# One layer in FP32: the first norm and its first twenty products as one region in a written order, the set-up placed later, and the values of both attention branches projected together

## The chip, the cores and the metric

The kernel runs on one core of one Trainium2 chip. The metric is the device time of one execution in microseconds (us); the median of several executions is given. Engines are called as in the profile: PE (TensorE, matmul; PEld are its weight loads, which overlap the matmuls), DVE (VectorE), ACT (ScalarE), POOL (GpSimd) and SP (SyncE, which issues most DMAs).

## The reference

The layer takes x (1024 tokens by 1024 columns, FP32) and computes

```
x = x + 1/2 * SwiGLU_1(RMSNorm(x))            # d_ff 2816
u = RMSNorm(x);  proj = u @ w_mix_in          # q,k,v of branch A, q,k,v of branch B, gate logits
A = chunked band attention (8 heads of 64)    # B = differential attention (4 heads, v of 128)
x = x + W_o( sigmoid(g_A) * (A W_A) + sigmoid(g_B) * (B W_B) )
x = x + 1/2 * SwiGLU_2(RMSNorm(x))
out = RMSNorm(x)
```

with `rms_norm(x, g) = x * rsqrt(mean(x*x) + eps) * g` and `swiglu(x) = (silu(x @ w_gate) * (x @ w_up)) @ w_out`. The values of the branches, `v_a` and `v_b`, are 512 columns of the projection each.

## The kernel before

Each large matrix product is done in a Strassen-like form: both operands are cut into 2 x 2 blocks and seven products (`PRODUCTS`, numbered m = 0 to 6) replace eight. The token side needs seven operands (`U_OPS`: A11, A12, S1 to S4, A22; S1 = A21 + A22, S2 = S1 - A11, S3 = A11 - A21, S4 = A12 - S2), the weight side four blocks and the differences T1, T2, T3, N4. Each FP32 operand is split (`split`, L97 and L102) into a rounded high part, cast by ACT, and a low part, subtracted by DVE; each block product is then three matmuls (`mm3`, L128 to L130: high by high, high by low, low by high).

A `Pair` takes two 128-column strips of an input projection (for the first SwiGLU one strip of the gate half and one of the up half). One product of a pair is four blocks of 128 rows, so 12 matmuls of 512 token columns. Its accumulators are chains in PSUM: chain "q" runs through m = 0, 3, 5, 6, "r" through 1 and 4, "s" is m = 2. `Combine` copies and adds what leaves the chains and hands the four result blocks to a sink. `ffn_in` has 22 pairs. The first five (`HEADS`) are begun with m = 0 and m = 2 alone (`head`), since these need only A11 and A12, the upper half of the tokens; the remaining products follow in `rest`, pair by pair. The sink applies silu to gate blocks (L401), multiplies (L409), and stores hidden blocks and their sums to DRAM; of a begun pair's gate block one is parked in DRAM (`begun`, `gb`).

The first norm, at the start, is in the code below: for each of eight row tiles of 128 tokens the row is loaded, ACT squares it with a running sum (`take`, L174), DVE adds eps (L180), POOL takes the power -1/2 (L139), DVE scales by root and gain (L181), PE transposes (L208), ACT and DVE split (`norm0`, `norm1a` to `norm1c`).

`setup` is a generator that `ffn_in` steps at pairs 5, 8, 11 and 14: lambda's four vectors and their dots (L651, L654), `subln_g`, the gate bias (transposed), then the tables of the two relative biases (POOL, L644) written to DRAM, which the attention stage reads. Its loads are issued on POOL's queue. `tc.issue_after(...)` around a step queues only its instructions of ACT's own queue behind the given silu.

`project_v` is called twice from `mixer_in`, once per branch, with one pair between. Each call cuts the 512 value columns into two of 256; the tokens are the stationary operand, the weights move, 256 columns at a time.

The order of the instructions on each engine is made by the framework's scheduler from data dependences, priorities and its own time estimate; nothing before the change is ordered by hand at the start. A region under `tc.manual_schedule(engines=...)` keeps, on each engine named, the order in which the code issues them; where other instructions fall among them is still the scheduler's. Buffers are rings by tag: ten raw tiles (`raw`), ten weight units (`w`, two for each split block), ten `f` temporaries, three `t`; PSUM has six `mm` banks and two `tr`.

Of the kernel before, what the change touches and what calls it, by code (L numbers as in the profile page):

```python
# [9 lines left out]
F32 = mybir.dt.float32  # L10
F32R = mybir.dt.float32r
AF = mybir.ActivationFunctionType
ALU = mybir.AluOpType
# [3 lines left out]
P = 128  # L17
# [28 lines left out]
WA = 640  # L46
EA = 768
WB = 1024
HEADS = 5
SKEW = 32  # L50
EB = 1152
# [3 lines left out]
def hybrid_layer_kernel(ctx, tc, x, ffn1_norm, ffn1_w_in, ffn1_w_out, mix_norm, w_mix_in,  # L55
# [306 lines left out]
            pass  # L362


    def ffn_in(w_in, u, ps, extra=None):
# [24 lines left out]

        begun = drams(HEADS, [P, HALF], "gb")
        keeps = []

        def make_sink(j):
            keep = {}
            keeps.append(keep)

            def sink(th, blk, ap):
                if blk == 0:
                    dst = temp([P, HALF], "gate") if th else ap  # L400
                    silu.append(nc.scalar.activation(out=dst, in_=ap, func=AF.Silu))  # L401
                    ap = dst
                if j < HEADS and (th, blk) == (0, 0):
                    nc.sync.dma_start(out=begun[j], in_=ap)
                    return
                keep[th, blk] = ap
                if (th, 0) in keep and (th, 1) in keep:
                    hid[j, th] = h = keep[th, 1]
                    nc.vector.tensor_tensor(out=h, in0=h, in1=keep[th, 0], op=ALU.mult)  # L409
                    hidden(j, th)  # L410
            return sink

        pairs = [Pair(w_in, j * P, FF + j * P, u, ps, make_sink(j)) for j in range(NF)]
        for p in pairs[:HEADS]:
            p.head()
            yield
        for j, p in enumerate(pairs):
            if j < HEADS:
                keeps[j][0, 0] = load(begun[j], temp([P, HALF], "gb"))
            if extra and j in (5, 8, 11, 14):  # L420
                with tc.issue_after(silu[-1].ins):
                    next(extra, None)
            p.rest()
# [214 lines left out]
    def setup(ps):  # L638

        def stage(shape, name):  # L640
            return sb.tile(shape, F32, tag="gain", bufs=1, name=name)
# [2 lines left out]
            nc.gpsimd.tensor_scalar(out=dst, in0=src, scalar1=-1.0, scalar2=None, op0=ALU.mult)  # L644


        for q, k in ((lambda_q1, lambda_k1), (lambda_q2, lambda_k2)):
            qk = []
            for v in (q, k):
                vt = small.tile([P, B_DIM], F32, tag="lv", bufs=2, name="lv")  # L650
                nc.gpsimd.dma_start(out=vt, in_=v[0].partition_broadcast(P))  # L651
                qk.append(vt)
            dot = small.tile([P, 1], F32, tag="dot", name="dot")
            nc.vector.tensor_tensor_reduce(out=qk[0], in0=qk[0], in1=qk[1], scale=1.0, scalar=0.0,  # L654
                                           op0=ALU.mult, op1=ALU.add, accum_out=dot)
            lams.append(dot)
        nc.gpsimd.dma_start(out=gsub, in_=subln_g[0].rearrange("(p o) -> p o", o=1))
        nc.gpsimd.tensor_scalar(out=gsub, in0=gsub, scalar1=1.0 - LAMBDA_INIT, scalar2=None, op0=ALU.mult)
        bg_rows = stage([16, P], "bg_rows")
        nc.gpsimd.dma_start(out=bg_rows, in_=b_gate[0].rearrange("(j p) -> j p", p=P))  # L660
# [14 lines left out]
        yield  # L675
        ea = stage([P, EA], "ea")
        n_clip = EA - (2 * REL_CLIP + 1)
        nc.gpsimd.dma_start(out=ea[:, n_clip:], in_=spread(rel_bias_a[0], A_HEADS, 2 * REL_CLIP + 1))
# [5 lines left out]
        nc.gpsimd.dma_start(out=tb, in_=spread(t5_bias, B_HEADS, 32))  # L684
# [9 lines left out]
    with tc.tile_pool(name="ps1", bufs=1, space=PSUM) as ps:  # L694

        u = new_u(U_OPS)
        ones = const.tile([1, P], F32, name="ones")
        nc.vector.memset(ones, 1.0)
        gain = sb.tile([P, D], F32, tag="gain", bufs=1, name="gain")
        for part in range(2):  # L700
            g_row = wtemp([1, HALF], "g_row")
            nc.scalar.dma_start(out=g_row, in_=ffn1_norm[0][part * HALF:(part + 1) * HALF].rearrange("(o d) -> o d", o=1))
            pg = ps.tile([P, HALF], F32, tag="mm", bufs=6, name="pg")
            nc.tensor.matmul(pg, ones, g_row, start=True, stop=True)
            nc.scalar.copy(out=halves(gain)[part], in_=pg)
        ffn1 = ffn_in(ffn1_w_in[0], u, ps, setup(ps))
        row0, row1 = [], []
        for t in range(4):
            row0.append(Row(load(rows(x)[t], raw_tile([P, D], "xt"))))
            row0[t].take()  # L710
            row0[t].scale(gain)
            norm0(t, row0[t], u, ps)
        next(ffn1, None)
        for t in range(4):
            row1.append(Row(load(rows(x)[4 + t], raw_tile([P, D], "xt"))))
            row1[t].take()
            row1[t].scale(gain)
            norm1a(t, row0[t], row1[t], u, ps)
        for _ in range(3):
            next(ffn1, None)  # L720
        for t in range(4):
            norm1b(t, row0[t], row1[t], u)
        next(ffn1, None)
        for t in range(4):
            norm1c(t, row1[t], u)
        run_all(ffn1)


        u2 = {}

        def project_v(br, c0):

            rw = [load(w_cols(w_mix, c0, HALF, 2 * r, 2), raw_tile([P, 2, HALF])) for r in range(4)]
            gets = [weight_ops({"B11": rw[q][:, :, :256], "B12": rw[q][:, :, 256:],
                                "B21": rw[2 + q][:, :, :256], "B22": rw[2 + q][:, :, 256:]},
                               [P, 2, 256]) for q in range(2)]

            def make_sink(a):
                def sink(th, blk, ap):
                    t0 = 4 * th + 2 * a  # L740
                    if (th, blk) == (1, 0):
                        o = temp([P, 2, 256], "vo")
                        nc.scalar.copy(out=o, in_=ap)
                        ap = o
                    nc.sync.dma_start(out=v_d[br][t0 * P:(t0 + 2) * P, blk * 256:(blk + 1) * 256].rearrange(
                        "(s p) c -> p s c", p=P), in_=ap)
                return sink
            ch = [Combine(ps, [P, 2, 256], make_sink(a)) for a in range(2)]
            for ms in ((0, 1), (2, 3), (4, 5), (6,)):
                ops = {}  # L750
                for a in range(2):
                    for m in ms:
                        an, bn, _ = PRODUCTS[m]
                        if a == 0:
                            ops[m] = [g(bn) for g in gets]
                        acc, first = ch[a].acc(m)
                        for s in range(2):
                            c = slice((2 * a + s) * P, (2 * a + s + 1) * P)
                            for k in range(4):

                                mm3(acc[:, s, :], [v[:, k, c] for v in u2[an]],
                                    [v[:, k % 2, :] for v in ops[m][k // 2]],
                                    first and s == 0 and k == 0, k == 3, not (first and s == 0))
                        ch[a].after(m, acc)

        def qk_sink(n):
            def sink(th, blk, ap):
# [18 lines left out]
        def mixer_in():  # L786
# [337 lines left out]
```

## Time and profile before

| what | value |
|---|---|
| time, median of 3 runs | 2111.92 us (2109.3 to 2114.98) |
| the profiled execution | 2110.54 us, its span 2108.7 us |
| mean granted TensorE clock | 0.994 |
| DMA | 324.61 MB, 153 GB/s of HBM over the span |

The span is the time between the first and the last instruction in the trace; the execution's own time lies a little above it. Rows of the trace name the line of the kernel, the engine and operation, and the tile written `<-` the tiles read.

### The profile page before, as it was taken

Reading aid. Unit: us, or ns where it says so; the run is one execution under the profiler, and the core shown is the slowest. Engines: PE = TensorE matmul, PEld = TensorE weight load, DVE = VectorE, ACT = ScalarE, POOL = GpSimd, SP = SyncE. Lnnn points to the kernel's source line nnn. Section 1 sums busy time; section 2 is a strip of 40 time slices with the busy share of each in tenths; the row PEclk is TensorE's granted clock in tenths of the full one; section 3 lists DMA queues with packets and bytes.
Section 4 is the critical chain, followed back from the end, with each engine's and each line's share of the span. In section 5 each row is a group of like instructions: output and inputs, shape, how many; then the busy total and the mean of one; then the engine's idle time right before and its main releaser. Section 6 shows DMA issues by size and latency. Waiting matters only on the chain.

```text
span 2108.7 us, 28259 instructions
## 1 busy us (share of the span) xinstructions
PE 2044.7 (97%) x9901; PEld 1699.8 (81%) x9901; DVE 1379.2 (65%) x2462; ACT 956.5 (45%) x1828; POOL 140.3 (7%) x202
## 2 busy tenths in 40 slices
PE   6899999999999999999999999999899999999998
PEld 4688888888888788899877888788688888888887
DVE  6765656658567855654656787568765656658566
ACT  6433333334446644433467666157433333334454
POOL 2300000000000000000036211000000000000000
PEclk9999999999999999999999999999999999999999
DMA  5743423366344744643495265734543323376335
GB/s 164 217 135 100 125 85 106 104 249 225 96 139 136 205 135 130 230 150 115 140 318 181 106 200 179 245 122 131 177 136 100 124 86 101 109 248 226 95 109 177
DMA packets 274580, 324.61 MB, mean 154 GB/s; under 512 B 15246, under 2 KB 170654, under 8 KB 274436
## 3 DMA queue, kind: packets, MB, share of 16 engines
q1 hardware_dynamic: 273248, 319.55, 46.4%
q0 software_dynamic: 1184, 3.24, 0.6%
q8 instruction: 78, 1.28, 0.2%
q14 instruction: 66, 0.54, 0.1%
q10 hardware_dynamic: 4, 0.00, 0.0%
HBM read 221.74 MB, written 100.99 MB: 153 GB/s over the span
## 4 chain that ended last, share of the span: by engine, by line
PE 88%; DVE 6%; issue 2%; ACT 2%; DMA 1%; POOL 0%; SPq 0%; POOLq 0%; DVEq 0%; ACTq 0%
PE prod L128 19%; PE prod L129 19%; PE prod L130 19%; PE po L129 7%; PE po L128 7%; PE po L130 7%; PE pt L859 2%; DVE wlo L102 1%; PE pv L943 1%; PE pb L128 1%; PE pb L129 1%; PE pb L130 1%; PE sc L843 1%; PE sc L844 1%; DVE B L113 1%
## 5 line engine op out<-in xcount | busy, mean ns | idle before, releaser
L129 PE MATMUL po<-wlo,whi 128*128 128x512 f32 x700 | 273.8, 391 | 1.8 <-DVE wlo L102 1.8
L130 PE MATMUL po<-whi,wlo 128*128 128x512 f32 x700 | 272.5, 390 | 0.0
L97 ACT CAST whi<-raw 128x512 fp32r<-128x512 f32 x200 | 124.1, 622 | 293.6 <-PE prod L129 223.7
L97 ACT CAST whi<-T 128x512 fp32r<-128x512 f32 x192 | 119.1, 622 | 260.5 <-PE prod L129 248.0
L113 DVE TENSOR_TENSOR c<-prod,c 128x512 f32<-128x512 f32 x190 | 130.9, 690 | 146.1 <-PE prod L130 132.6
L97 ACT CAST whi<-B 128x512 fp32r<-128x512 f32 x175 | 109.0, 623 | 243.4 <-PE po L129 236.3
L102 DVE TENSOR_TENSOR wlo<-T,whi 128x512 fp32r<-128x512 f32 x192 | 131.8, 688 | 115.8 <-ACT whi L97 104.3
L102 DVE TENSOR_TENSOR wlo<-B,whi 128x512 fp32r<-128x512 f32 x175 | 120.4, 688 | 128.4 <-ACT whi L97 128.4
L102 DVE TENSOR_TENSOR wlo<-raw,whi 128x512 fp32r<-128x512 f32 x200 | 137.4, 688 | 92.7 <-ACT whi L97 59.9
L128 PE MATMUL po<-whi 128*128 128x512 f32 x700 | 189.5, 390 | 0.0
L129 PEld LDWEIGHTS po<-wlo,whi 128*128 128x128 f32 x700 | 131.5, 188 | 30.9 <-DVE wlo L102 4.0
L130 PEld LDWEIGHTS po<-whi,wlo 128*128 128x128 f32 x700 | 131.5, 188 | 27.0
L128 PEld LDWEIGHTS po<-whi 128*128 128x128 f32 x700 | 131.1, 188 | 27.2 <-ACT whi L97 0.2
L139 POOL TENSOR_TENSOR r<-v,neg_half 128x1 f32<-128x1 f32 x32 | 26.4, 830 | 1363.7 <-DVE v L180 1291.6
L102 DVE TENSOR_TENSOR wlo<-N,whi 128x512 fp32r<-128x512 f32 x64 | 44.2, 690 | 108.4 <-PE prod L129 69.0
L102 DVE TENSOR_TENSOR wlo<-ha,whi 128x512 fp32r<-128x512 f32 (+1 forms) x157 | 105.7, 674 | 11.7 <-ACT whi L97 11.5
L287 ACT COPY c<-prod 128x512 f32<-128x512 f32 x186 | 102.1, 585 | 17.2 <-issue 10.5
L97 ACT CAST whi<-ha 128x512 fp32r<-128x512 f32 (+1 forms) x157 | 95.2, 608 | 25.5 <-PE po L129 13.0
L128 PE MATMUL prod<-A11h,whi 128*128 128x512 f32 x240 | 96.1, 401 | 7.9 <-DVE c L113 6.7
L853 ACT ACTIVATE pm<-pm,mn 128x640 f32<-128x640 f32 (+7 forms) x128 | 93.9, 735 | 20.3 <-DVE mn L851 17.6
L128 PE MATMUL prod<-A12h,whi 128*128 128x512 f32 x240 | 94.6, 394 | 3.4 <-DVE c L113 3.4
L851 DVE CUSTOM_DVE_ANT_0 pm<-sc,nb 128x640 f32<-128x640 f32 (+7 forms) x128 | 87.5, 701 | 14.9 <-PE sc L844 9.6
(245 smaller groups left out, 5108.0 us busy)
## 6 DMA issues: line engine op xcount, KB each, us to landing
raw<-in_ffn_w_in_dram SPq DMA_DIRECT2D x98, 512.0 KB, 4.2
raw<-in_w_mix_in_dram SPq DMA_DIRECT2D x47, 512.0 KB, 4.6
ha<-hS SPq DMA_DIRECT2D x88, 256.0 KB, 2.6
hA<-c SPq DMA_DIRECT2D x66, 256.0 KB, 4.2
ha<-hA SPq DMA_DIRECT2D x55, 256.0 KB, 2.7
B<-in_ffn_w_out_dram SPq DMA_DIRECT2D x12, 1024.0 KB, 12.1
hS<-hs SPq DMA_DIRECT2D x44, 256.0 KB, 2.4
hS<-c SPq DMA_DIRECT2D x44, 256.0 KB, 4.2
```

What stands on the lines that cost most here:

```text
L97: nc.scalar.copy(out=hi, in_=src)
L102: (nc.gpsimd if on_pool else nc.vector).tensor_tensor(out=lo, in0=src, in1=h, op=ALU.subtract)
L113: nc.vector.tensor_tensor(out=out_, in0=a, in1=b, op=op)
L128: nc.tensor.matmul(ps, a[0], b[0], start=first, stop=False, skip_group_check=shared)
L129: nc.tensor.matmul(ps, a[0], b[1], start=False, stop=False, skip_group_check=shared)
L130: nc.tensor.matmul(ps, a[1], b[0], start=False, stop=last, skip_group_check=shared)
L139: nc.gpsimd.tensor_tensor(out=r, in0=v, in1=neg_half, op=ALU.pow)
L287: nc.scalar.copy(out=self.held[name], in_=p)
L843: nc.tensor.matmul(sc[:, m, :wc], qs[:, h, c], ks[:, h, kc], start=True, stop=False)
L851: nc.vector.tensor_tensor_reduce(out=d3, in0=sc, in1=nb.rearrange("p (n w) -> p n w", n=n), scale=1.0, scalar=3e38, op0=ALU.add, op1=ALU.m ...
L853: nc.scalar.activation(out=dst, in_=dst, func=AF.Exp, bias=mn, scale=-1.0, accum_out=rs)
L859: nc.tensor.transpose(pt[:, b, :], p, ident)
```

## The change

In `ffn_in`, a function `begin` does the first norm, the two products of each of the five begun pairs and all other products of pairs 0 and 1, in the order of a written list of tokens; the loop skips a pair that has nothing left to do. Each token is one step: `sq:t` square, `rt:t` root, `sc:t[:n]` scale (of half n, for rows 0 to 3), `tr`/`tm:t:n` transpose half n into a `tr` or `mm` bank, `hi`/`lo` the split of A11 or A12, `kp` the copy of a turned half, `s1` to `s4` the sums, `hX`/`lX` the split of operand X, `wh`/`wl:n:m` the split of pair n's weight of product m, `t:n:m` its difference, `p:n:m` product m of pair n, `copy`, `add`, `out` what leaves the accumulators, `open:n` the loads of pair n's four blocks, `gate:n` the parked gate block. The sum with eps is now POOL's, the copies of the gain DVE's, and the gain's spread over 128 partitions uses two rows of the identity instead of a row of ones.

```diff
@@ constants
+BEGIN = """
+pg:0 pg:1 g:0 sq:0 rt:0 g:1 sq:1 rt:1 sc:0:0 sq:2 rt:2 sc:0:1 tr:0:0 sc:1:1 sq:3 rt:3 tr:0:1
+sc:1:0 hi:0:0 tm:1:1 sc:2:0 wh:0:0 lo:0:0 tm:1:0 hi:0:1 sc:3:1 kp:0:0 tm:2:0 lo:0:1 wh:1:0 sq:4
+rt:4 sc:2:1 tr:3:1 wl:0:0 tm:2:1 kp:2:0 sc:3:0 kp:1:0 wl:1:0 tm:3:0 hi:2:0 sc:4 kp:3:1 hi:1:0
+lo:2:0 hi:3:0 tm:4:1 hi:2:1 lo:1:0 tm:4:0 hi:3:1 lo:3:0 kp:4:1 lo:3:1 p:1:0 sq:6 rt:6 s1:0
+lo:2:1 wh:2:0 s3:0 wh:2:2 wl:2:0 hi:1:1 sc:6 sq:5 rt:5 p:0:0 wh:3:2 lo:1:1 kp:3:0 wl:2:2 wh:4:2
+wl:3:2 wh:4:0 tr:6:1 sc:5 p:3:2 wh:1:2 sq:7 rt:7 wl:4:0 s2:0 hS1:0 kp:2:1 lS1:0 tm:5:1 hS2:0
+wl:1:2 tm:5:0 kp:0:1 lS2:0 kp:5:1 tr:6:0 s3:1 wh:3:0 p:1:2 s3:2 hS3:0 hS3:1 sc:7 kp:6:1 kp:1:1
+s1:2 copy:1:0 tr:7:0 s1:1 hS1:2 p:2:0 add:1:2 hA22:2 s3:3 hS1:1 out:1:2 lS1:2 hS3:3 lS1:1 hA22:1
+lS3:3 p:2:2 copy:2:0 lA22:1 wh:0:2 wl:3:0 copy:0:0 wl:0:2 hA22:0 hS3:2 s2:2 p:3:0 lS3:0 hS2:2
+s4:2 lS2:2 hS4:2 add:2:2 s2:1 tr:7:1 out:2:2 p:0:2 wl:4:2 copy:3:0 s4:1 kp:7:1 open:0 hS2:1
+add:3:2 hS4:1 s1:3 out:3:2 lS2:1 p:4:2 hS1:3 s2:3 hA22:3 add:0:2 hS2:3 t:0:5 wh:0:4 out:0:2
+gate:0 t:0:1 p:4:0 lS2:3 t:0:3 wh:0:5 lS1:3 wh:0:3 wl:0:4 wh:0:1 wl:0:3 copy:4:0 wl:0:1 p:0:3
+add:4:2 wl:0:5 out:4:2 lA22:2 s4:0 p:0:1 lS4:1 copy:0:3 lS3:2 hS4:0 lS3:1 lA22:3 lS4:0 p:0:5
+copy:0:1 s4:3 open:1 gate:1 lA22:0 hS4:3 lS4:2 lS4:3 t:0:6 p:0:4 add:0:5 out:0:5 wh:0:6 t:1:1
+wh:1:4 wl:0:6 wh:1:1 t:1:3 p:0:6 wl:1:1 wh:1:3 wl:1:4 wl:1:3 t:1:5 t:1:6 p:1:3 wh:1:5 add:0:4
+out:0:6 wh:1:6 wl:1:5 out:0:4 wl:1:6 p:1:1 copy:1:3 p:1:5 copy:1:1 p:1:4 add:1:5 out:1:5 p:1:6
+add:1:4 out:1:4 out:1:6
+"""
@@ ffn_in
         pairs = [Pair(w_in, j * P, FF + j * P, u, ps, make_sink(j)) for j in range(NF)]
-        for p in pairs[:HEADS]:
+        if begin:
+            begin(pairs, keeps, begun)
+        for p in pairs[:0 if begin else HEADS]:
             p.head()
             yield
         for j, p in enumerate(pairs):
+            if not p.todo:
+                continue
@@ the start
+            def root(t):
+                v, r = (small.tile([P, 1], F32, tag=n, name=n) for n in "vr")
+                nc.gpsimd.tensor_scalar(out=v, in0=row[t].ssq[:, 0:1], scalar1=EPS, scalar2=None, op0=ALU.add)
+                nc.gpsimd.tensor_tensor(out=r, in0=v, in1=neg_half, op=ALU.pow)
+                row[t].r = r
...
+            def open_pair(n):
+                r1, r2 = (pairs[n].load(i) for i in range(2))
+                blocks[n] = {"B11": r1[:, :4], "B21": r1[:, 4:], "B12": r2[:, :4], "B22": r2[:, 4:]}
+                src[n, 4] = blocks[n]["B22"]
...
+            def weight_hi(n, m):
+                ops[n, m] = [unit([P, 4, P], v) for v in ("whi", "wlo")]
+                nc.scalar.copy(out=ops[n, m][0], in_=src[n, m])
...
+            def multiply(n, m):
+                acc[n, m], first = pairs[n].sums.acc(m)
+                for k in range(4):
+                    mm3(acc[n, m], [v[:, k, :] for v in ops[n, m]], [v[:, k, :] for v in u[PRODUCTS[m][0]]],
+                        first and k == 0, k == 3, not first)
+                pairs[n].todo.remove(m)
...
+            with tc.manual_schedule(engines={getattr(mybir.EngineType, e)
+                                             for e in ("Activation", "DVE", "PE", "Pool", "SP")}):
+                open_rows(0, 1, 2, 3)
+                half_load(0, 0)
+                half_load(1, 0)
+                open_rows(4, 5)
+                half_load(0, 2)
+                half_load(1, 2)
+                open_rows(6, 7)
+                half_load(2, 0)
+                half_load(2, 2)
+                for n in (3, 4):
+                    r = pairs[n].load(0)
+                    src[n, 0], src[n, 2] = r[:, :4], r[:, 4:]
+                for token in BEGIN.split():
+                    op, *args = token.split(":")
+                    do[op](*map(int, args))
```

In `setup` all loads move from POOL's queue to ACT's and so fall under `issue_after`; the first step now only loads, the dots, `gsub` and the gate bias come with the second.

```diff
+        rows_ = []
         for q, k in ((lambda_q1, lambda_k1), (lambda_q2, lambda_k2)):
             for v in (q, k):
-                vt = small.tile([P, B_DIM], F32, tag="lv", bufs=2, name="lv")
-                nc.gpsimd.dma_start(out=vt, in_=v[0].partition_broadcast(P))
+                vt = small.tile([P, B_DIM], F32, tag="lv", bufs=4, name="lv")
+                nc.scalar.dma_start(out=vt, in_=v[0].partition_broadcast(P))
+                rows_.append(vt)
+        nc.scalar.dma_start(out=gsub, in_=subln_g[0].rearrange("(p o) -> p o", o=1))
...
+        nc.scalar.dma_start(out=bg_rows, in_=b_gate[0].rearrange("(j p) -> j p", p=P))
+        yield
```

The values of both branches are one 2 x 2 block form with the branches as the two column blocks, called once; each matmul moves 512 columns. One product needs the split weights of four row blocks, eight units.

```diff
+            rw = {(r, c): load(w_cols(w_mix, (VA, VB)[c], HALF, 2 * r, 2), raw_tile([P, 2, HALF]))
+                  for r, c in ((0, 0), (1, 0), (2, 0), (3, 0), (0, 1), (1, 1), (2, 1), (3, 1))}
...
+            for m in (0, 2, 1, 4, 3, 5, 6):
+                an, _, chain = PRODUCTS[m]
+                w = [split_units(weight(m, k)) for k in range(4)]
+                for t in range(4):
+                    shared = chain == "q" and m > 0
+                    acc = q[t] if shared else bank()
+                    for k in range(4):
+                        mm3(acc, [v[:, k, t * P:(t + 1) * P] for v in u2[an]], w[k],
+                            not shared and k == 0, k == 3, shared)
...
-                if n in (10, 11):
+                if n == 10:
                     flush()
-                    project_v(n - 10, (VA, VB)[n - 10])
+                    project_v()
```

More of the change, by code (lines that the diff above doesn't have):

```diff
@@ L362, in run_all, with ffn_in @@
             pass
-    def ffn_in(w_in, u, ps, extra=None):
+    def ffn_in(w_in, u, ps, extra=None, begin=None):
         silu, hid = [], {}
@@ L673, in write_rows @@
                 nc.gpsimd.dma_start(out=diag[:, c * r:(c + 1) * r, e0:e1], in_=src)
-        yield
         ea = stage([P, EA], "ea")
         n_clip = EA - (2 * REL_CLIP + 1)
-        nc.gpsimd.dma_start(out=ea[:, n_clip:], in_=spread(rel_bias_a[0], A_HEADS, 2 * REL_CLIP + 1))
+        nc.scalar.dma_start(out=ea[:, n_clip:], in_=spread(rel_bias_a[0], A_HEADS, 2 * REL_CLIP + 1))
         negate(ea[:, n_clip:], ea[:, n_clip:])
@@ L683, in setup @@
         tb = small.tile([P, 32], F32, tag="tb", bufs=1, name="tb")
-        nc.gpsimd.dma_start(out=tb, in_=spread(t5_bias, B_HEADS, 32))
+        nc.scalar.dma_start(out=tb, in_=spread(t5_bias, B_HEADS, 32))
         for e0, e1 in ((0, EB - HALF), (EB - HALF, EB)):
@@ L696, in hybrid_layer_kernel @@
         u = new_u(U_OPS)
[L697 to L725, printed above, removed]
+        def begin(pairs, keeps, begun):
+            row, tr, src, ops, acc, held, s1, blocks = [], {}, {}, {}, {}, {}, {}, {}
+            gain = sb.tile([P, D], F32, tag="gain", bufs=1, name="gain")
+            g_row = wtemp([2, HALF], "g_row")
+            nc.scalar.dma_start(out=g_row, in_=ffn1_norm[0].rearrange("(n d) -> n d", n=2))
+            pg = {}
+            def spread_gain(n):
+                pg[n] = ps.tile([P, HALF], F32, tag="mm", bufs=6, name="pg")
+                nc.tensor.matmul(pg[n], ident[:2, n:n + 1].to_broadcast([2, P]), g_row, start=True, stop=True)
+            def root(t):
[3 more added lines that the diff above has]
+                row[t].r = r
+            def scaled(t, n=None):
+                c = slice(0, D) if n is None else slice(n * HALF, (n + 1) * HALF)
+                nc.vector.scalar_tensor_tensor(out=row[t].x[:, c], in0=row[t].x[:, c], scalar=row[t].r,
+                                               in1=gain[:, c], op0=ALU.mult, op1=ALU.mult)
+            def turn(t, n, tag="tr"):
+                tr[t, n] = ps.tile([P, 4, P], F32, tag=tag, bufs=2 if tag == "tr" else 6, name="tr")
+                for k in range(4):
+                    nc.tensor.transpose(tr[t, n][:, k, :], halves(row[t].x)[n][:, k * P:(k + 1) * P], ident)
+            def kept(t, n):
+                return by_k(halves(row[t].x)[n])
+            def part(name, t):
+                return [v[:, :, t * P:(t + 1) * P] for v in u[name]]
+            def high(name, t, s):
+                nc.scalar.copy(out=part(name, t)[0], in_=s)
+            def low(name, t, s):
+                h, l = part(name, t)
+                add(l, s, h.bitcast(F32), ALU.subtract)
+            def first_sum(t):
+                s1[t] = temp([P, 4, P], "s1")
+                add(s1[t], tr[t + 4, 0], kept(t + 4, 1))
+            def operand(name, t):
+                return {"S1": lambda: s1[t], "S2": lambda: kept(t, 0), "S4": lambda: kept(t, 1),
+                        "S3": lambda: kept(t + 4, 0), "A22": lambda: kept(t + 4, 1)}[name]()
+            def open_pair(n):
+                r1, r2 = (pairs[n].load(i) for i in range(2))
+                blocks[n] = {"B11": r1[:, :4], "B21": r1[:, 4:], "B12": r2[:, :4], "B22": r2[:, 4:]}
+                src[n, 4] = blocks[n]["B22"]
+            def gate(n):
+                keeps[n][0, 0] = load(begun[n], temp([P, HALF], "gb"))
+            def difference(n, m):
+                a, b = {1: ("B12", "B11"), 3: ("B22", 1), 5: ("B22", "B12"), 6: ("B21", 3)}[m]
+                src[n, m] = wtemp([P, 4, P], "T")
+                add(src[n, m], blocks[n][a], blocks[n][b] if isinstance(b, str) else src[n, b], ALU.subtract)
+            def weight_hi(n, m):
+                ops[n, m] = [unit([P, 4, P], v) for v in ("whi", "wlo")]
+                nc.scalar.copy(out=ops[n, m][0], in_=src[n, m])
+            def weight_lo(n, m):
+                add(ops[n, m][1], src[n, m], ops[n, m][0].bitcast(F32), ALU.subtract)
+            def multiply(n, m):
[4 more added lines that the diff above has]
+                pairs[n].todo.remove(m)
+            def copied(n, m):
+                held[n, m] = temp([P, HALF], "c")
+                nc.scalar.copy(out=held[n, m], in_=acc[n, m])
+            def added(n, m):
+                h = held[n, {2: 0, 4: 3, 5: 1}[m]]
+                add(h, acc[n, m], h)
+            def given(n, m):
+                th, blk = {2: (0, 0), 4: (0, 1), 5: (1, 1), 6: (1, 0)}[m]
+                pairs[n].sums.sink(th, blk, acc[n, 6] if m == 6 else held[n, {2: 0, 4: 3, 5: 1}[m]])
+            do = {"pg": spread_gain, "g": lambda n: nc.vector.tensor_copy(out=halves(gain)[n], in_=pg[n]),
+                  "sq": lambda t: row[t].take(), "rt": root, "sc": scaled, "tr": turn,
+                  "tm": lambda t, n: turn(t, n, "mm"),
+                  "hi": lambda t, n: high(("A11", "A12")[n], t, tr[t, n]),
+                  "lo": lambda t, n: low(("A11", "A12")[n], t, tr[t, n]),
+                  "kp": lambda t, n: nc.scalar.copy(out=kept(t, n), in_=tr[t, n]),
+                  "s1": first_sum,
+                  "s3": lambda t: add(kept(t + 4, 0), kept(t, 0), tr[t + 4, 0], ALU.subtract),
+                  "s2": lambda t: add(kept(t, 0), s1[t], kept(t, 0), ALU.subtract),
+                  "s4": lambda t: add(kept(t, 1), kept(t, 1), kept(t, 0), ALU.subtract),
+                  "open": open_pair, "gate": gate, "t": difference, "wh": weight_hi, "wl": weight_lo, "p": multiply,
+                  "copy": copied, "add": added, "out": given}
+            for name in ("S1", "S2", "S3", "S4", "A22"):
+                do["h" + name] = lambda t, name=name: high(name, t, operand(name, t))
+                do["l" + name] = lambda t, name=name: low(name, t, operand(name, t))
+            def half_load(n, m):
+                src[n, m] = load(w_cols(pairs[n].w, pairs[n].c[0], P, 2 * m, 4), temp([P, 4, P], "wraw"))
+            def open_rows(*ts):
+                for t in ts:
+                    row.append(Row(load(rows(x)[t], raw_tile([P, D], "xt"))))
+            with tc.manual_schedule(engines={getattr(mybir.EngineType, e)
[15 more added lines that the diff above has]
+                    do[op](*map(int, args))
@@ L726, in hybrid_layer_kernel @@
+        ffn1 = ffn_in(ffn1_w_in[0], u, ps, setup(ps), begin)
         run_all(ffn1)
         u2 = {}
[L731 to L764, printed above, removed]
```

47 lines of the change are left out of this document (41 added, 6 removed).

## The prediction

> **What bounds the kernel now.** I read the engine table, then the work of each engine in stretches, then the instructions in order of time at the start and in the values stage, last the waits.
>
> ```profile
> span 2108.7 us, 28259 instructions
> PE 2044.7 (97%) x9901; PEld 1699.8 (81%) x9901; DVE 1379.2 (65%) x2462; ACT 956.5 (45%) x1828; POOL 140.3 (7%) x202
> 0.00:100.00 100.00, 72.92 (x301) 55.63 (x302) 67.72 (x115) 55.84 (x101) 32.06 (x60) 0.97 0.64 189
> 40.00:80.00 40.00, 32.44 (x146) 25.66 (x144) 36.72 (x60) 25.42 (x45) 6.96 (x7) 0.91 0.66 190
> 100.00:160.00 60.00, 60.00 (x266) 49.70 (x265) 39.44 (x62) 21.59 (x38) 0.00 (x0) 1.00 0.45 144
> 1010.00:1060.00 50.00, 50.00 (x223) 41.41 (x222) 30.71 (x48) 21.53 (x38) 0.00 (x0) 1.00 0.53 189
> ```
>
> In the last four rows the columns are the stretch, its length, then busy time (count) of PE, PEld, DVE, ACT and POOL, the granted clock, DMA share, GB/s. PE is busy 97% of the span, so only PE work or PE idle time that goes can shorten the run. Of 64 us of idle PE, 27 lie in the first 100; right behind, PE is full. From 40 to 80 VectorE is busy 36.7 of 40: there the norm is held by DVE.
>
> ```profile
> 4.35 1.06 ACT L174 ACTIVATE junk<-xt 128x1024 bf16<-128x1024 f32 x1 [1.53 <-DMA xt<-in_x_dram]
> 9.81 0.23 DVE L654 CUSTOM_DVE_ANT_0 lv<-lv 128x64 f32<-128x64 f32 x1 [4.13 <-DMA lv<-in_lambda_k_dram]
> 10.08 0.20 ACT L813 ACTIVATE le<-dot 128x1 f32<-128x1 f32 x1 [2.57 <-DVE dot L654]
> 31.01 0.80 PE L128 MATMUL prod<-A11h,whi 128*128 128x512 f32 x1 [0.68 <-ACT A11h L97]
> 34.52 0.40 PE L128 MATMUL prod<-A11h,whi 128*128 128x512 f32 x1
> 61.62 0.80 PE L128 MATMUL prod<-A12h,whi 128*128 128x512 f32 x1 [3.37 <-DVE c L113]
> 76.51 0.50 PE L128 MATMUL prod<-S1h,whi 128*128 128x512 f32 x1 [1.15 <-DVE c L113]
> ```
>
> Here a row is start, duration, engine, line, operation, with the wait before it in brackets. The first row of x is squared at 4.35, but DVE then stands 4.13 us behind a set-up load (lambda), and ACT 2.57 behind DVE. The first product starts at 31.01. PE stands again before 61.62, and last before 76.51.
>
> **The change, part by part.** It is three edits: the region, the set-up, the values.
>
> *Region.* It holds 20 products (both of each begun pair, the other five of pairs 0 and 1) of 12 matmuls, the same 20 that the old kernel does first. Prices:
>
> ```profile
> 0.00:100.00 100.00, 32.05 (x78) 0.97 0.64 189
> 862.43 0.39 PE L128 MATMUL prod<-S1h,whi 128*128 128x512 f32 x1
> 865.15 0.39 PE L128 MATMUL prod<-A12h,whi 128*128 128x512 f32 x1
> 40.49 0.60 PE L208 MATMUL tr<-ident,xt 128*128 128x128 f32 x4
> 40.84 0.47 PE L128 MATMUL prod<-A11h,whi 128*128 128x512 f32 x1
> 51.27 0.69 DVE L102 TENSOR_TENSOR S1l<-s,S1h 128x512 fp32r<-128x512 f32 x1
> 57.29 0.68 DVE L113 TENSOR_TENSOR xt<-xt,tr 128x512 f32<-128x512 f32 x1
> 11.90 3.67 DVE L181 SCALAR_TENSOR_TENSOR xt<-xt,r,gain 128x1024 f32<-128x1024 f32 x3 [0.39 <-ACT gain L705]
> 14.87 1.06 ACT L174 ACTIVATE junk<-xt 128x1024 bf16<-128x1024 f32 x1
> 15.92 0.57 ACT L97 CAST A12h<-tr 128x512 fp32r<-128x512 f32 x1
> 47.09 1.14 ACT L97 CAST A22h<-xt 128x512 fp32r<-128x512 f32 x2
> L139 POOL TENSOR_TENSOR r<-v,neg_half 128x1 f32<-128x1 f32 x32 | 26.4, 830 | 1363.7 <-DVE v L180 1291.6
> L658 POOL TENSOR_SCALAR gsub<-gsub 128x1 f32<-128x1 f32 x1 | 0.9, 902 | 0.0
> GB/s 0 47 315 322 332 74 82 397 410 293 272 333 391 414 371 391 389 325 296 281 188 1 0 0 0 0 53 315 164 0 0 0 0 0 0 0 0 0 132 345
> raw<-in_ffn_w_in_dram SPq DMA_DIRECT2D x98, 512.0 KB, 4.2
> ```
>
> The first row counts the matmuls of L128 alone in the first 100 us: 78, so 78 of the 80 triples are done. A product is 12 steps, 865.15 - 862.43 = 2.72 us; two more triples are 1.4. The old kernel ends the 20 products at 101.4.
>
> Durations for the new one: a DVE operation of 512 columns in a row of them every (57.29 - 51.27)/10 = 0.60 us, one of 1024 columns 3.67/3 = 1.2 or two units; a square on ACT 15.92 - 14.87 = 1.05, a cast about 0.52; a turn of four transposes 0.35.
>
> First product. The eight loads of x and ten of weights are 6.5 MB. The GB/s row gives the moved KB of each of the first us (40 slices of 1 us): 2.1 MB, the first four rows, by about 9.4, 5.6 MB by 20. The first square ends at 5.4. The root now takes two operations on POOL, 0.90 + 0.83 (bounds: 0.15, as the sum costs on DVE now, and the 0.90 of the other row; I take the POOL row, the same engine), so the first scaling may start at 7.1. Up to `lo:3:0`, the last thing `p:1:0` needs, DVE does 19 units, 11.4 us, so 18.5; row 3's square and root hold it up to 1 us. ACT's 16 operations to `hi:3:0`, five of them squares, are 11.0 us from 4.4 and are done earlier. First product: 19.5, 11.5 us sooner.
>
> PE behind it: 20 x 2.72 = 54.4; 1.8 for the slow start (31.01 to 34.52 ran at half speed, 3.5 us lost by half); six more turns, 2.1. Sum 58.3, end 77.8 without a gap.
>
> Is DVE ahead of that? Its units to `wl:0:3` are 70, 51 after `lo:3:0`: 19.5 + 51 x 0.60 = 50.1, and the eleventh product could start on PE at 19.5 + 1.8 + 27.2 + 2.1 = 50.6. To `lS4:3` 84 units, 58.5; its product 58.8. So DVE and PE end nearly together, with 0.3 to spare, and DVE's own waits come out on PE. I can name three: ACT's ninth weight cast waits for a unit (five pairs of them) that `p:1:2` holds, and `copy:1:0` and `add:1:2` stand behind it, 1.4; `t:0:5` needs pair 0's second block, whose buffer is free when `wl:4:2` (unit 57, 42.3) is done, plus 0.4 issue and 4.2 landing, 46.9 against 45.9, so 1.0; late rows 0.6. Together 3.0 - 0.3 = 2.7, end 80.5. Gain 101.4 - 80.5 = 20.9 us. Bounds: 23.6 with no wait; 11 if waits are as in the second rival.
>
> Moves inside: eight small sums leave DVE for POOL and two gain copies come to it from ACT: 8 x 0.15 against 2 x 0.60, nothing. The gain's matmul now waits for the identity, which POOL makes without the set-up's issues ahead of it: nothing. What follows the region (pair 2's blocks) may be issued among the region's SP instructions; in the sum PE has no hole there. The cover is the three units of slack DVE has at the end (unit 97, `wl:1:6`, at 66 to 70, before the last product at 78); without it, see the first rival.
>
> *Values.* Before, 672 matmuls of 256 columns (21 forms of 32); after, 336 of 512.
>
> ```profile
> L128 PE MATMUL prod<-whi,A11h 128*128 128x256 f32 x32 | 9.1, 283 | 0.0
> 898.67 0.28 PE L129 MATMUL prod<-wlo,A11h 128*128 128x256 f32 x1
> 901.07 0.28 PE L128 MATMUL prod<-whi,S1h 128*128 128x256 f32 x1
> 905.00:925.00 20.00, 20.00 (x169) 20.00 (x168) 7.40 (x12) 8.24 (x15) 0.00 (x0) 1.00 0.24 83
> ```
>
> Twenty steps take 2.40 us, 0.120 each, and PEld is busy 20.00 of 20: the weight loads set the pace. 672 x 0.120 = 80.6; 336 x 0.2267 = 76.2. PE is full there, so all 4.4 us count. Casts, differences and stores stay the same work in other shapes. New is that one product takes eight of ten weight units: of the next one's four pairs, one is free beforehand, the others as the last token tile passes them, 2.04, 1.36 and 0.68 us before the end. The last is cast and subtracted (0.52 + 0.69) by about 1.0 after the end and needed at 2.04: no stall. If that cover is gone see the third rival. Eight of ten raw buffers are held as well; two free with `b22`, two products before the end, so the next pair's load (4.2) is covered.
>
> The Trainium skill, TensorE: Matmul & The Clock Gate, "Wait — 56ns, not 53.3ns?", has a matmul step as columns over 2.4 GHz plus 2.5 ns, so 109 and 216 ns, and by it the joint form would save 0.9 us (estimate). The trace disagrees with both steps (120 and 227), and its full PEld row says why at 256 columns.
>
> *Set-up.* Its loads go from POOL's queue to ACT's, behind a silu of a begun pair's rest; the dots, the bias rows and 30 POOL operations come after.
>
> ```profile
> 0.74 0.76 ACTq L702 DMA_DIRECT2D g_row<-in_ffn_norm_dram  x2
> L174 ACT ACT_TABLE_LOAD x1 | 1.3, 1283 | 1.5 <-PEq L1110 1.5
> L644 POOL TENSOR_SCALAR eb<-tb 128x1 f32<-128x1 f32 (+9 forms) x30 | 12.0, 431 | 14.7 <-issue 8.9 <-DMA diag_b<-eb 5.8
> ACT whi L97 <- PE prod L129: 572.2, 339, 4.6
> ```
>
> What it takes off the start is in the first-product sum. Later it costs ACT eight issues of 0.38, 3.0 us, and the two exponentials of lambda, which now fall among the silus, two to four table loads, 2.6 to 5.1. ACT is busy 21.5 of 50 and its casts mostly wait for PE to free a unit (last row), so they are ahead and hide it; uncovered it would be 8 us. POOL's work has its first reader in the attention stage, behind 1080. I take nothing.
>
> **The sum.** 20.9 + 4.4 = 25.3. The profiled execution took 2110.5 (span 2108.7 and 1.8 around it), so 2085.2; the median of the runs is 1.4 above it, 2086.6. I say 2087.
>
> **The rivals.**
>
> ```profile
> 42.38 0.63 ACT L401 ACTIVATE c<-c 128x512 f32<-128x512 f32 x1
> 84.96 0.68 DVE L409 TENSOR_TENSOR c<-c,gb 128x512 f32<-128x512 f32 x1
> ```
>
> *A hole behind the region.* If pair 2's blocks are issued behind the region's last stores, PE waits for silu 0.63, product 0.68, four sums 2.4, issue 0.4, landing 4.2, cast 0.52, difference 0.69: 9.5, and 1.8 of slow clock. For it: SP is one of the ordered queues, and raw buffers are short there. Against it: nothing in the code binds a load outside. 2087 + 11 = 2098.
>
> *The written order stands.* Every engine waits for its next token though others are ready. It decides at (101.4 - 80.5 + 4.4)/95 = 0.27 us more per DVE operation: then nothing is left. With 0.4, 38 us, the time is 2125, slower. For it: DVE and PE run neck and neck. Against: the order puts rows and weights in the sequence in which the loads come. At 0.1 the end is 2097.
>
> *Values stall.* If the next weights begin only when a product is over, each of six changes costs a cast and four differences, 3.0: 18 us, 2105. For it: eight of ten units. Against: the timing above.
>
> *No change.* DVE's work is the same, so if its first 20 us can't be filled, the end stays about where it is: only the values' 4.4, 2107. Against it: its early waits are set-up's, not data's.
>
> *Values save little.* If PE's step went with the columns alone, half as many matmuls of double width would take the same time: 2091. Against it: 0.120 is more than half of 0.2267. By the skill's step above it would be 2090.5.
>
> **How the numbers follow.** My forecast 0.58, values that save little 0.05; the hole 0.13; an order that stands but still gains (2097) 0.06; values 0.07; no change 0.05; slower 0.06. About 0.3%, 6.3 us, is what a measurement of this kernel can tell from no change, so 2105.6 to 2118.2 is "same". No change and half of the values case make 0.08, slower 0.06, faster 0.86. Low: no waits (2.7 less) and a like amount in stalls elsewhere, with 3 for the reordering of all that follows, 2079. High: hole and order, with their 3, 2101; values, no change and slower stay out, 0.18.
>
> **What would show it.** Region: the first product near 19.5, not 31; 80 triples done by about 81; DVE busy over 0.8 from 20 to 66; no wait of SP before pair 2's blocks. Values: 336 matmuls of 512 columns 0.227 apart, PEld well under 100%, no PE wait on a cast at the six changes. Set-up: no lambda load before 100, ACT table loads behind it with PE full. I am wrong if PE idles over 12 us between 20 and 80, or if a hole stands at the region's end.

## The result and the profile after

The changed kernel takes 2092.83 us in the median (2090.58 to 2095.17, 4 runs) against 2112.18 for the kernel before on the same chip: 19.4 us less, ratio 0.991, 95% interval 0.9898 to 0.9921. The profiled execution took 2095.17, the slowest of the four; its stages are compared here with the 2110.54 of the profile before.

First the page's span and PE line, then the stretches that were shown of before, in the same columns.

```profile
span 2093.4 us, 27563 instructions
PE 2042.2 (98%) x9565; PEld 1685.2 (81%) x9565; DVE 1381.9 (66%) x2463; ACT 956.2 (46%) x1824; POOL 135.3 (6%) x202
0.00:100.00 100.00, 89.01 (x379) 70.82 (x380) 80.17 (x127) 59.31 (x107) 9.39 (x22) 0.95 0.69 205
40.00:80.00 40.00, 36.90 (x155) 29.48 (x154) 34.98 (x59) 20.41 (x37) 0.00 (x0) 0.96 0.77 211
100.00:160.00 60.00, 58.34 (x257) 47.62 (x256) 35.85 (x62) 22.44 (x39) 0.29 (x1) 1.00 0.31 100
```

PE is busy 89 of the first 100 us instead of 73. New are 1.7 us of idle PE between 100 and 160, where it was full.

Next, PE at the places that the prediction named, from the order of time of the kernel after.

```profile
19.94 0.78 PE L147 MATMUL prod<-A11h,whi 128*128 128x512 f32 x1
43.99 0.47 PE L147 MATMUL prod<-A12h,whi 128*128 128x512 f32 x1 [0.68 <-DVE c L132]
54.43 0.50 PE L147 MATMUL prod<-S2h,whi 128*128 128x512 f32 x1 [2.00 <-ACT whi L785]
55.59 0.50 PE L149 MATMUL prod<-S2h,wlo 128*128 128x512 f32 x1 [0.42 <-DVE wlo L132]
57.44 0.63 PE L149 MATMUL prod<-S2h,wlo 128*128 128x512 f32 x1
59.58 0.62 PE L148 MATMUL prod<-S1l,whi 128*128 128x512 f32 x1
0.00:84.00 84.00, 32.80 (x80) 0.94 0.69 200
```

The first product starts at 19.94 instead of 31.01. PE then runs almost closed up to 52, waits 2.00 and 0.42, and falls to half speed: five steps from 57.44 take 0.43 us each instead of 0.227, and the granted clock from 57 to 60 is 0.50. The last row counts the matmuls of one line up to 84.0: the 80 triples of the region's 20 products are done there.

Last, the stages. A row gives, for all instructions of one form, the shortest, median and longest duration in ns, then the start of the first and of the last: the first output matmul of the first SwiGLU, and the first and last attention score. Before:

```profile
L128 PE MATMUL po<-whi x700: 387/389/477, 458.3 to 2069.8; 128*128 128x512 f32 x175
L843 PE MATMUL sc<-ks,qs x192: 220/364/505, 1078.6 to 1303.1; 128*128 128x320 f32 x80, 128*128 128x384 f32 x32, 128*128 128x512 f32 x32, 128*128 128x128 f32 x16
```

And after:

```profile
L147 PE MATMUL po<-whi x700: 387/389/477, 442.8 to 2054.1; 128*128 128x512 f32 x175
L987 PE MATMUL sc<-ks,qs x192: 220/365/688, 1058.7 to 1286.9; 128*128 128x320 f32 x80, 128*128 128x384 f32 x32, 128*128 128x512 f32 x32, 128*128 128x128 f32 x16
```

Up to the first output matmul 458.3 - 442.8 = 15.5 us are gained. From there to the first score the stage takes 615.9 instead of 620.3, 4.4 less: the values. From the first to the last score it takes 228.2 instead of 224.5, 3.7 more in these two executions; the last section says what the traces show of that.

The values stage after, in the columns of the stretches:

```profile
905.00:925.00 20.00, 20.00 (x90) 16.57 (x89) 10.89 (x18) 7.11 (x12) 0.00 (x0) 1.00 0.25 79
L147 PE MATMUL prod<-whi,A12h 128*128 128x512 f32 x16 | 6.2, 397 | 0.3 <-DVE vh L132 0.3
```

PEld is busy 16.57 of 20 instead of 20.00, and the only wait of PE while the values are multiplied is the 0.3 us in the second row (16 matmuls of 512 columns where there were 32 of 256).

### The profile page after: what moved, and what is told of

It reads as the page before. It is cut to its first block, busy times and chain, and to the rows that moved or that the text cites. A ratio compares the mean times of both kernels' runs of the same rounds, so it can differ in the third digit from the quotient of the medians.

```text
span 2093.4 us, 27563 instructions
## 1 busy us (share of the span) xinstructions
PE 2042.2 (98%) x9565; PEld 1685.2 (81%) x9565; DVE 1381.9 (66%) x2463; ACT 956.2 (46%) x1824; POOL 135.3 (6%) x202
## 4 chain that ended last, share of the span: by engine, by line
PE 88%; DVE 5%; issue 2%; ACT 2%; DMA 1%; POOL 0%; SPq 0%; ACTq 0%; DVEq 0%; POOLq 0%
PE prod L147 19%; PE prod L148 19%; PE prod L149 19%; PE po L148 7%; PE po L147 7%; PE po L149 7%; PE pt L1003 2%; PE pv L1087 1%; PE pb L147 1%; PE pb L148 1%; PE pb L149 1%; DVE wlo L121 1%; PE sc L987 1%; PE sc L988 1%; PE pv L1151 1%
## 5 line engine op out<-in xcount | busy, mean ns | idle before, releaser
L116 ACT CAST whi<-T 128x512 fp32r<-128x512 f32 x174 | 108.1, 623 | 230.5 <-PE prod L148 221.8
L132 DVE TENSOR_TENSOR c<-prod,c 128x512 f32<-128x512 f32 x178 | 122.9, 691 | 133.6 <-PE prod L149 122.1
L121 DVE TENSOR_TENSOR wlo<-T,whi 128x512 fp32r<-128x512 f32 x174 | 119.6, 689 | 102.1 <-ACT whi L116 101.8
L116 ACT CAST whi<-ha 128x512 fp32r<-128x512 f32 (+1 forms) x157 | 95.4, 609 | 25.3 <-PE po L148 12.8
L121 DVE TENSOR_TENSOR wlo<-N,whi 128x512 fp32r<-128x512 f32 x58 | 40.0, 690 | 99.9 <-PE prod L148 63.5
L997 ACT ACTIVATE pm<-pm,mn 128x640 f32<-128x640 f32 (+7 forms) x128 | 93.9, 735 | 21.5 <-DVE mn L995 19.1
L147 PE MATMUL prod<-S2h,whi 128*128 128x512 f32 x240 | 94.2, 392 | 3.0 <-ACT whi L785 2.0
L149 PE MATMUL prod<-A11h,wlo 128*128 128x512 f32 x240 | 95.7, 399 | 0.0
L148 PE MATMUL prod<-A11l,whi 128*128 128x512 f32 x240 | 95.6, 398 | 0.0
```

The costliest lines, as they stand in the source:

```text
L116: nc.scalar.copy(out=hi, in_=src)
L121: (nc.gpsimd if on_pool else nc.vector).tensor_tensor(out=lo, in0=src, in1=h, op=ALU.subtract)
L132: nc.vector.tensor_tensor(out=out_, in0=a, in1=b, op=op)
L147: nc.tensor.matmul(ps, a[0], b[0], start=first, stop=False, skip_group_check=shared)
L148: nc.tensor.matmul(ps, a[0], b[1], start=False, stop=False, skip_group_check=shared)
L149: nc.tensor.matmul(ps, a[1], b[0], start=False, stop=last, skip_group_check=shared)
```

## The experiments

All ratios are to the kernel before on the same chip, with their 95% intervals. The chip is not the same in all runs, so two versions are compared by their ratios, or by what each takes less than its own kernel before; the changed kernel has 0.991 (0.9898 to 0.9921) and 19.4 us less. "First output" is the start of the first output matmul of the first SwiGLU, "values stage" the time from it to the first score, both from the profiled execution.

**One edit alone, one edit undone.** The joint values in the old kernel:

> The kernel before with the joint values alone. Theory (the edits add up, values as costed): 672 steps of 0.120 us become 336 of 0.2267 with no wait between products, 4.4 us less than before, ratio 0.998. Rival (the step goes with the columns alone): within 1 us of before. Rival (weight units stall the six changes of product): up to 14 us more than before.

Measured: 2108.89 against 2112.11, ratio 0.9984 (0.9975 to 0.9993), 3.2 us less; first output 458.0, values stage 616.4 against 620.3. This is the theory, with 3.9 of its 4.4 us in the stage. PE doesn't wait for a weight cast there, so the values don't stall.

```diff
 # e2_region_setup: the kernel after, with the two old calls
-                if n == 10:
+                if n in (10, 11):
                     flush()
-                    project_v()
+                    project_v(n - 10, (VA, VB)[n - 10])
```

> The changed kernel with the values projected twice as before. Theory: only the 4.4 us of the values are lost against the changed kernel, so 14 to 16 us less than before, ratio about 0.993; the first attention score then comes about 15.5 us earlier than before. Rival (the edits help each other): 10 us or less below before.

Measured: 2092.55, ratio 0.9904 (0.9891 to 0.9918), no slower than the changed kernel: the theory had 14 to 16 us less than before, the rival 10 or less, and it is 19.6. In its stages the values do count, 618.4 against 615.9, but the start is 1.8 us better (first output 441.0), and its first score at 1059.4 is 19.2 earlier than before, not 15.5. The 1.8 us are in the main the half-speed stretch: PE waits 1.78 instead of 2.00 at the same place, and stays at full speed. So against the changed kernel the values are worth 2.5 us in the stage. Over the profiled executions of all versions the stage takes 618.4 to 620.3 with the values apart (three versions) and 614.5 to 616.5 with them together (eleven), so the gain there is real. In the whole time of this pair it doesn't show, and what gives it back is not settled; in the two profiled executions the rest, from the first score on, is 1027.7 here and 1034.7 in the changed kernel.

The later set-up alone (`setup` as after, in the old kernel):

> The kernel before with the later set-up alone (the gain is spread with a row of the identity). Theory: the start loses the wait of 4.1 us on lambda's vectors, but the norm stays bound by VectorE and the later set-up costs 1.7 us of PE idle near 125: between 0 and 3 us less than before. Rival (the set-up is what the gain at the start is made of): 8 us or more below before.

Measured: 2111.70, ratio 0.9993 (0.9984 to 1.0002). The first product comes at 27.91, 3.1 us earlier, the first output only 0.7 earlier. So the set-up did stand in the way of the start, but most of the start's gain lies elsewhere.

The old `setup` in the changed kernel:

> The changed kernel with the set-up as before, its loads on POOL's queue and free to go early. Theory (the later set-up costs 1.7 us at 120 to 140 through ACT's blocked issues and two table loads, and the region by itself keeps its gain unless set-up work stands in its queues): about equal to the changed kernel, -2 to +3 us. Rival (the set-up in the first 10 us is what held the start): the first product some 4 us later and the time 4 us or more above the changed kernel.

Measured: 2094.82, ratio 0.9914 (0.9901 to 0.9928), first product 21.4, first output 444.3. PE is busy 60.00 of the 60 us from 100 to 160, and waits 2.51 before 71.98 instead. The two kernels are equal within the intervals: another place of the set-up moved the loss, it didn't remove it.

**The written order.** Only the region's header goes; the scheduler orders each engine from the same trace.

```diff
-            with tc.manual_schedule(engines={...}):
+            if True:
```

> The changed kernel with the same code in the same sequence, but without the ordered region: the scheduler orders each engine. Theory (the order per engine is what moves the first products): the first product comes later than 20 us, and 8 us or more of the region's 15 to 17 are lost. Rival (the gain comes from what was rewritten: half rows, half weight loads, root on POOL, all of pairs 0 and 1 traced together): within 4 us of the changed kernel.

Measured: 2093.00, ratio 0.9918 (0.9904 to 0.9931), first product 20.5, first output 443.6. This is the rival: the order per engine, the visible half of this change, is worth 0.8 us by the first output, and nothing that the ratios can tell. What then moved the start? Two more runs change this kernel. In the first its 233 steps are traced in the sequence of the kernel before:

> The same 233 steps with the same operations, traced in the sequence of the kernel before (row by row, begun pairs between the norm's parts, then pairs 0 and 1), without the ordered region. Theory (the gain at the start is the sequence in which the steps are traced, which the scheduler takes as its priority): the first product later than 25 us, the first output matmul of the first SwiGLU 8 us or more later than the 443.6 of the kernel without region. Rival (the gain is in the rewritten operations and banks): within 3 us of 443.6.

Measured: 2095.12, ratio 0.9924 (0.9911 to 0.9936), first product 19.1, first output 445.1. The sequence in which the steps are traced isn't it either: 1.5 us. In the second all turns (a turn is the four transposes of half a row) go to the two `tr` banks:

```diff
-                  "tm": lambda t, n: turn(t, n, "mm"),
+                  "tm": lambda t, n: turn(t, n),
```

> The changed kernel without the ordered region and with every transpose in the two tr banks of PSUM, as before, none in the mm banks. Theory (two banks hold the transposes behind the copies and differences that read them): the first product 2 to 5 us later than 20.5, the first output matmul of the first SwiGLU 2 to 5 us later than 443.6. Rival (the roots on POOL and the rows set the start): within 1 us.

Measured: 2107.14, ratio 0.9978 (0.9969 to 0.9987), first product 29.55, first output 456.6. With all transposes in two banks the first product comes 9.1 us later and the start is nearly the old one, a larger loss than the theory gave. What PE waited for up to its first product (total us, times, longest), in the kernel before:

```profile
PE tr L208 <- ACT xt L219: 9.6, 5, 2.9
PE tr L208 <- DVE xt L181: 7.1, 1, 7.1
PE pg L704 <- DMA g_row<-in_ffn_norm_dram: 2.2, 1, 2.2
```

In the kernel after:

```profile
PE tr L747 <- DVE xt L741: 4.6, 5, 1.4
PE pg L731 <- DMA g_row<-in_ffn_norm_dram: 3.3, 1, 3.3
```

After, with two banks only:

```profile
PE tr L747 <- ACT xt L814: 6.0, 3, 2.6
PE tr L747 <- DVE xt L741: 4.1, 2, 3.7
PE pg L731 <- DMA g_row<-in_ffn_norm_dram: 3.3, 1, 3.3
PE tr L747 <- DVE A11l L132: 3.0, 2, 1.9
```

`ACT xt` is the copy that empties a bank for the next transpose. In the kernel before PE waits 9.6 us for it, in five pieces. After, nine of the sixteen turns go to `mm` banks, seven of them listed ahead of the first product, when no product uses these banks yet: the wait is gone. With two banks it is back (6.0, and 3.0 on the differences that read the same banks). So 13.0 of the first output's 14.7 us (456.6 - 443.6 of 458.3 - 443.6) hang on the tag of these turns. That is shown in the new code; the old code with more banks was not run.

**The loss at 54.** DVE and ACT both stop there for pair 0's blocks. These are the issues on SP, and what waits, in the kernel after (the first row is two issues, of which the second waits for its silu):

```profile
37.82 7.06 SPq L423 DMA_DIRECT2D gb<-c  x2
44.98 1.13 SPq L138 DMA_DIRECT2D raw<-in_ffn_w_in_dram  x2
44.36 0.69 DVE L132 TENSOR_TENSOR wlo<-raw,whi 128x512 fp32r<-128x512 f32 x1
51.23 1.29 DVE L132 TENSOR_TENSOR T<-raw 128x512 f32<-128x512 f32 x2 [2.58 <-DMA raw<-in_ffn_w_in_dram]
```

Two things end at 45: the second store of a parked gate block, ahead of `open:0` on SP, and `wl:4:2`, which frees the second buffer. Each was moved alone, then both (there `open:0` is listed ahead of `add:2:2`, which for SP is the same place).

```diff
-... add:2:2 s2:1 tr:7:1 out:2:2 ... kp:7:1 open:0 hS2:1        # open: loads ahead of the store
+... add:2:2 s2:1 tr:7:1 open:0 out:2:2 ... kp:7:1 hS2:1
-... wl:3:0 copy:0:0 ... p:0:2 wl:4:2 copy:3:0                  # wl: buffer free earlier
+... wl:3:0 wl:4:2 copy:0:0 ... p:0:2 copy:3:0
```

> The changed kernel with the loads of pair 0's blocks moved in SP's order ahead of the store of out:2:2, nothing else. Theory (the 2.0 us wait of PE at 54.4 comes from these loads standing behind a store that waits for a silu): the first block lands at about 45 and the second 2 us earlier than now; PE's wait shrinks by 1 to 2 us. Rival (the second block's buffer, free only when wl:4:2 is done, sets it): no change of the wait.

> The changed kernel with wl:4:2 moved in VectorE's order right behind wl:3:0, so that the raw buffer is free some 4 us earlier; the loads stay behind the store. Theory (the store sets it): both loads are still issued near 45, no gain. Rival (the buffer sets it): loads some 4 us earlier, PE's wait at 54.4 and the slow clock behind it gone, 3 to 4 us less.

> The changed kernel with both moves. Theory (both conditions, store and buffer, bind at nearly the same time): loads issued by 41, landed by 47, no wait of PE at 54.4, no half clock behind it: 3.5 to 4.5 us less than the changed kernel. Rival (VectorE is the bound at that place anyway): under 1.5 us less.

Measured, in this order: 2092.17 (0.9906, 0.9893 to 0.992), 2093.65 (0.9915, 0.9901 to 0.9928), 2086.45 (0.9888, 0.9874 to 0.9901); first output 439.0, 442.3, 438.6. Freeing the buffer alone changes nothing (PE waits 1.94, and the half speed stays): the store holds both loads. The loads ahead of the store take PE's 2.0 us wait and the half speed away, 3.8 us by the first output; the whole times don't show it, 18.4 us less than before against 19.4. Both together give 4.2 by the first output and are 24.1 us less than before, so 4.7 better than the changed kernel, with intervals that just overlap. PE of the first 100 us with both:

```profile
0.00:100.00 100.00, 91.30 (x396) 72.80 (x397) 82.64 (x131) 60.63 (x109) 10.08 (x22) 0.97 0.71 208
```

**The loss at 131.** ACT after, with its queue's DMA issues (`ACTq`), and the two waits of PE:

```profile
123.57 0.42 ACTq L674 DMA_DIRECT2D lv<-in_lambda_k_dram  x1
126.74 0.33 ACTq L676 DMA_DIRECT2D gsub<-in_subln_g_dram  x1
128.65 0.34 ACTq L678 DMA_DIRECT2D bg_rows<-in_b_gate_dram  x1
129.09 0.59 ACT L306 COPY c<-prod 128x512 f32<-128x512 f32 x1 [4.96 <-DMA lv<-in_lambda_k_dram]
130.21 1.28 ACT L957 ACT_TABLE_LOAD   x1
132.33 1.28 ACT L420 ACT_TABLE_LOAD   x1
131.72 0.20 PE L687 MATMUL trb<-ident,bg_rows 16*128 16x16 f32 x1 [0.74 <-DMA bg_rows<-in_b_gate_dram]
135.34 0.50 PE L147 MATMUL prod<-A11h,whi 128*128 128x512 f32 x1 [0.92 <-ACT whi L116]
```

After four lambda loads the fifth issue comes 2.7 us late on ACT's queue and the sixth, the gate bias, behind it; ACT's own work stands behind both, 4.96 us in all. Then come two table loads, one for lambda's exponentials and one back for silu. PE idles 0.74 for the gate bias, which it transposes, and 0.92 for a weight cast. In the test lambda's loads go to POOL at the very start, dots and exponentials into the region.

```diff
+                load_lambda()                       # four loads on POOL
                 open_rows(0, 1, 2, 3)
...
-... s2:0 hS1:0 ... tm:5:0 kp:0:1
+... s2:0 dot:0 dot:1 hS1:0 ... tm:5:0 exp:0 exp:1 kp:0:1
```

> The changed kernel with lambda's four loads on POOL's queue at the start, its dots on VectorE behind s2:0 and its two exponentials on ACT behind hS2:0, inside the region; the rest of the set-up as in the changed kernel. Theory (the 1.7 us of PE idle near 131 to 135 come from lambda's loads blocking ACT's queue and from the two table loads of the exponentials): no ACT table load and no PE wait between 120 and 145, 1.5 to 2 us less than the changed kernel. Rival (the loads at the start delay the rows): first product 1 us or more later, no gain.

> The changed kernel with lambda early and with both moves of the pair-0 loads. Theory (the two losses are separate): 5 to 6 us less than the changed kernel, near 2086 to 2087, first output matmul of the first SwiGLU near 437. Rival (VectorE takes the time back): no better than the pair-0 moves alone.

Measured: 2088.58 (0.9889, 0.9875 to 0.9902), first output 439.1; with the pair-0 moves 2087.80 (0.9884, 0.9869 to 0.9899), 438.1. In both PE is busy 60.00 of 60 from 100 to 160, with no table load there: the theory of the 1.7 us holds. Lambda early alone gains more than that, 3.7 by the first output, because PE's wait before 53.78 is 1.59 there and the half-speed stretch is gone too. The pair-0 moves take the same stretch away, so the two fixes don't add up: against the changed kernel they give 4.7 by the first output, where the theory had 5 to 6, against the pair-0 moves alone 0.5, and the ratios of these two, 0.9884 and 0.9888, can't be told apart. Of the 1.4 us that PE idles from 100 to 160 with the pair-0 moves alone, 0.9 are lost again before the first product, which starts at 20.45 instead of 19.54. The third row of x shows where, its square on ACT and its scaling on DVE, here with both fixes:

```profile
10.00 1.06 ACT L193 ACTIVATE junk<-xt 128x1024 bf16<-128x1024 f32 x1 [3.08 <-DMA xt<-in_x_dram]
12.14 0.75 DVE L730 SCALAR_TENSOR_TENSOR xt<-xt,r,gain 128x512 f32<-128x512 f32 x1 [1.48 <-POOL r L725]
```

and here with the pair-0 moves alone:

```profile
8.16 1.06 ACT L193 ACTIVATE junk<-xt 128x1024 bf16<-128x1024 f32 x1 [0.74 <-DMA xt<-in_x_dram]
10.74 0.75 DVE L741 SCALAR_TENSOR_TENSOR xt<-xt,r,gain 128x512 f32<-128x512 f32 x1 [0.46 <-POOL r L736]
```

The row lands later, and DVE waits for its root. In the three versions with lambda's loads at the start (lambda early, both fixes, and the old `setup` in the changed kernel) this square begins at 9.1 to 10.0, in the eight others with the new start at 7.3 to 8.7. That agrees with the rival, loads at the start that delay the rows, but it is not shown by itself, and with lambda early alone the first product is no later (19.70). By their ratios both versions are 4 to 6 us faster than the changed kernel; between them the runs can't tell.

## Why the prediction was right, and where not

*Bound and place: right.* PE's idle time in the first 100 us fell from 27 to 11, and in the values the weight loads no longer fill the time.

*First product: 19.5 predicted, 19.94 measured, for a partly wrong reason.* The sum of DVE's units held, because the new list keeps DVE fed:

```profile
6.11 0.57 POOL L736 TENSOR_TENSOR r<-v,neg_half 128x1 f32<-128x1 f32 x1
7.04 0.69 DVE L809 COPY gain<-pg 128x512 f32<-128x512 f32 x1 [1.01 <-PE pg L731]
7.65 2.73 DVE L741 SCALAR_TENSOR_TENSOR xt<-xt,r,gain 128x512 f32<-128x512 f32 x4
18.19 1.88 DVE L132 TENSOR_TENSOR A11l<-tr,A11h 128x512 fp32r<-128x512 f32 x3
```

The last row ends with `lo:3:0` at 20.07, where the sum had 19.5, and the second matmul, the first that reads a low part, starts at 20.52. That it is so near is in part luck. The root, priced at 0.90 + 0.83 on POOL, took 0.25 + 0.57 for the first row (the bound from DVE was the nearer) and was done at 6.68; but the first scaling waited for the copies of the gain until 7.65, a path that the prediction had put at nothing.

The prediction put what stood in the way before on the set-up ("its early waits are set-up's, not data's"), and the later set-up alone gives 3.1 of the 11.1 us. For the rest the run with two banks points to PE's wait for a free PSUM bank: it puts the first product back to 29.55. The step that failed is that the prediction read DVE's 4.13 us in the order of time and left out the list of waits of the first 31 us, where the copy that empties a bank stands first with 9.6; of the tokens `tm` it said nothing.

*Region's end: 80.5 predicted, 84 measured.* The mis-sized term is the wait of `t:0:5` for pair 0's second block, put at 1.0. It was priced by the buffer alone, with the landing of one load; the store ahead of `open:0` on SP was overlooked, and two loads issued together landed at 51.2, not 46.9. PE lost 2.42 us in waits and about 1.6 at half speed (eight steps from 56.62 to 60.00 in 3.4 instead of 1.8). Of the other two waits that were named, 1.4 and 0.6, PE shows one of 0.68 behind the first product, before 43.99.

*Set-up: nothing predicted, 1.7 us measured.* The cover was there for table loads and issues as busy time; that an issue can stand, and ACT's casts and the gate bias behind it, wasn't counted.

*Values: 4.4 predicted, 4.4 in the stage between the two profiles, 3.9 alone, 2.5 when undone.* The timing of the weight units held: no product waits for a weight.

*Sum.* 25.3 were predicted; 15.5 + 4.4 = 19.9 are measured up to the first score, and 19.4 between the medians, so the time lies 5.8 us above the forecast of 2087. What is missing is the wait at 54 with its half speed and the set-up's 1.7. Of the rivals, the hole at the region's end didn't come (PE is full from 60 to 120), nor a stall of the values. The rival of a standing order has one true instance, the store ahead of the loads, with 4 us instead of its 10 and more.

## What to carry to other kernels

Before a start is rewritten into an order by hand, read the waits of that stretch by engine: what freed each wait names the resource, and here more banks for the transposes gave nearly all that the order seemed to give. In a written order, every DMA queue counts as an engine: look at what waits ahead of each load, and at what stands behind an issue on an engine that also computes.

## What the hardware showed that was not expected

The clock of PE halved after waits of 2.00 and 0.42 us within some 3 us, and not after 1.78 and 0.42 at the same place. The Trainium skill, TensorE: Matmul & The Clock Gate, "HAM oscillation — how this bites in real kernels", gives about 3.4 us of idle time as the rule. Here less was enough, and the half-speed stretch was 3.4 us long. A threshold can't be read from these runs: after a single wait of 2.14 before 48.67, in the run with the old sequence, the clock halved as well, and after the single 2.51 before 71.98, in the run with the old `setup`, it didn't.

Such borderline waits are also in the attention stage. In the profile of after PE waits 2.72 us before 1224.55, and the granted clock from 1225 to 1250 is 0.88; in the profile of before it is 1.00 from 1200 to 1300, and the whole stage takes 3.7 us less. With the values projected twice as before, and the new start, the clock is 1.00 there too and the stage takes 223.7; in the kernel before with the later set-up alone it takes 227.2. So the 3.7 us lie where executions differ, and nothing here makes them a cost of the change; what brings the wait about was not tried.

Whole executions of one kernel differ in the same way: the one with both pair-0 moves took 2091.2 at a mean granted clock of 0.992, and 2085.6 to 2086.7 at 0.995 to 0.996. Differences of 2 to 5 us between single executions go with the clock; which waits make them was not tried by itself.
